# A transformer block on one core: another order for the first transfers, dummy products and transposes

## The chip, the cores and the metric

The kernel runs on one core of a Trainium2 chip. The metric is the device time of one execution, in microseconds; lower is better. Five engines work side by side, each through its own queue in order: TensorE (PE; its weight loads are listed as PEld), VectorE (DVE), ScalarE (ACT), GpSimd (POOL) and SyncE (SP), which only issues transfers here. Transfers from HBM to the on-chip memory are issued by SP, ScalarE or GpSimd and carried by the core's 16 DMA engines.

## What is computed

One layer of a trunk with two token mixers in parallel, float32, 256 tokens of width 2048, with 16 learned meta tokens in front of them:

```
h = concat(meta, x)                              # (16 + 256, 2048)
u = rms_norm(h, g_pre_mix)
z_pool, v_conv, g_conv, gate_a, gate_b = split(u @ w_in)   # 1024 1024 1024 2048 2048
y_a = causal_multiscale_pool(z_pool, w_pool_grp, pool_scale) @ w_pool_out
y_b = conformer_conv(v_conv, g_conv, ...) @ w_conv_out
m = sigmoid(gate_a) * y_a + sigmoid(gate_b) * y_b
h = h + rms_norm(m @ w_o, g_post_mix)
u = rms_norm(h, g_pre_mlp)
h = h + rms_norm(relu(u @ w_up)**2 @ w_down, g_post_mlp)
return h[16:]
```

The change touches the preparation of `u` and the first products of `u @ w_in` alone.

## The kernel before

**Precision.** Each float32 weight is split into a rounded high part `hi` (cast on ScalarE, L250) and the rest `lo` (subtraction on VectorE, L253), each activation likewise into `u[..., 0, :]` and `u[..., 1, :]`; a product is hi·hi + hi·lo + lo·hi, three matmuls (`mm3`, L422).

**Streaming.** All weights come as chunks of 1 MB from one list, `stream`, into three rotating buffers `raw`. Each of the first chunks is 8 row groups of 128 by 256 columns of `w_in`, so two chunks hold the 16 row groups (k = 0 to 15) of the first 256 columns. `open_chunk` issues a chunk's transfers; for the first two chunks its argument says how many row groups go in each transfer and on which queue. `pieces_to` splits single row groups of the first three chunks into hi and lo.

**The start.** The order is written out by hand; nothing is scheduled afterwards, so each engine does its instructions in the order of the program. Transfers: SP loads the meta tokens (`m_in`, 16 rows of 8 KB) and ScalarE the gains `g_pre_mix`; then `x` comes in four blocks of 512 columns (block b holds k = 4b to 4b + 3), block 0 with its first 128 tokens on SP and the others on ScalarE; then chunk 0 (one row group on ScalarE, then one, two, two, two on SP), x block 1 on ScalarE, x block 2 on SP, chunk 1 on SP, x block 3 on SP; the small vectors and the conv taps on GpSimd. ScalarE then loads a function table (`warm_up`).

TensorE begins with `keep_warm(8)`, transposes of the identity into a tile `idle` that nobody reads; then `meta_tokens` transposes the meta rows, 16 pieces of 16 by 128, and the gains (`rows_to_columns`, L312), multiplies on VectorE and casts on ScalarE; then `keep_warm(4)`.

**The loop** (L525 to L540) runs k from -4 to 15. For negative k it transposes one x tile each (`x_tile`, two transposes of 128 by 128, L370, called xt0 to xt3 in the text), scales it into `u` (ScalarE L371, VectorE L372) and splits one row group of weights. From k = 0 on it multiplies row group k into two accumulators `acc_v` (six matmuls of 272 columns, called product k), and after each odd k transposes the next two x tiles. So TensorE's order is xt0 to xt3, products 0 and 1, xt4, xt5, products 2 and 3, xt6, xt7, and so on. The norm's factor is applied later, from sums of squares (`sq_tile`), for which the meta rows are read untransposed from `m_in`.

Of the kernel before, what the change touches and what calls it, by code (L numbers as in the profile page):

```python
# [8 lines left out]
F32 = mybir.dt.float32  # L9
F32R = mybir.dt.float32r  # L10
AF = mybir.ActivationFunctionType
# [3 lines left out]
P = 128  # L15
CK = 4
CW = 512
# [83 lines left out]
def hybrid_block(ctx: ExitStack, tc: tile.TileContext, ins: dict, out: bass.AP):  # L101
    nc = tc.nc
    x = ins["x"][0]
    meta = ins["meta"]
    T, D = x.shape
    M = meta.shape[0]
    L = M + T
    NT = T // P
    KD = D // P
# [17 lines left out]
    const = ctx.enter_context(tc.tile_pool(name="const", bufs=1))  # L127
# [3 lines left out]
    tmp = ctx.enter_context(tc.tile_pool(name="tmp", bufs=2))  # L131
# [3 lines left out]
    def f32(ap):  # L135
        return ap.bitcast(F32)

    def acc_tile(name):
        return psA.tile([P, CW], F32, tag="acc", name=name)

    def misc_tile(name):
        return psB.tile([P, CW], F32, tag="misc", name=name)
# [43 lines left out]
    HALF = (2 * CK, CW // 2)  # L186
# [24 lines left out]
    opened = []  # L211
# [13 lines left out]
    def part_tile(tag, n, standing=False):  # L225

        key = f"{tag}{n % 3}"
        room = ready.pop(key) if key in ready else part_room(key, f"{tag}_{n}")
        place = 2 if standing and tag == "hi" else 1
        shift = (place - 1 - 3 * KEYS.index(key)) % 4 * LINE  # L230
        return room[:, shift:shift + CK * CW]

    def open_chunk(first=((2, nc.sync),) * 4):
        n = at["n"]
        at["n"] += 1
        src, (rows, width) = stream[n]
        raw = raws.tile([P, CK * CW], F32, tag="raw", name=f"raw_{n}")
        hi, lo = (part_tile(tag, at["parts"], n in standing_chunks) for tag in ("hi", "lo"))
        at["parts"] += 1
        flat, (raw, hi, lo) = raw, (t.rearrange("p (k c) -> p k c", k=rows) for t in (raw, hi, lo))  # L240
        pieces = rows if n < FIRST + 1 else 1
        k = rows // pieces
        i = 0
        for n_, queue in first if n < FIRST else ((rows, nc.sync),):
            sl = slice(i, i + n_)
            queue.dma_start(raw[:, sl, :], src[:, sl, :])
            i += n_

        def high(sl):
            nc.scalar.copy(hi[:, sl, :], raw[:, sl, :])  # L250

        def low(sl):
            nc.vector.tensor_sub(lo[:, sl, :], raw[:, sl, :], f32(hi[:, sl, :]))  # L253

        def piece(i):
            def f():
                sl = slice(i * k, (i + 1) * k)
                high(sl)
                low(sl)
            return f  # L260
        opened.append((hi, lo, [piece(i) for i in range(pieces)], flat))
# [13 lines left out]
        return opened.pop(0)[:2]  # L275


    ident = const.tile([P, P], F32, name="ident")
    make_identity(nc, ident)
    ones = const.tile([P, P], F32, name="ones")  # L280
# [3 lines left out]
    def warm_up(func):  # L284

        nc.scalar.activation(warm, ones[:, 0:1], func)
# [3 lines left out]
    m_in = big.tile([M, D], F32, tag="a", name="m_in")  # L290
# [9 lines left out]
    def load_rows(queue, *names):  # L300
        rows = tmp.tile([48, P], F32, tag="g", name=f"rows_{names[0]}")
        n = 0
        for name in names:
            v = ins[name][0].rearrange("(k p) -> k p", p=P)
            queue.dma_start(rows[n:n + v.shape[0], :], v)
            n += v.shape[0]
        return rows, n, names[0]

    def rows_to_columns(rows, n, name):

        pv = misc_tile(f"pv_{name}")
        nc.tensor.transpose(pv[:, :n], rows[:n, :], ident[:n, :n])  # L312
        nc.vector.tensor_copy(vecs[:, cols[name]:cols[name] + n], pv[:, :n])

    def col(name, k):
        return vecs[:, cols[name] + k:cols[name] + k + 1]

    def load_x(queue, b, ts=slice(0, NT)):
        sl = slice(b * CW, (b + 1) * CW)
        queue.dma_start(x_in[:, ts, sl], xv[:, ts, sl])  # L320


    nc.sync.dma_start(m_in, meta)
    pre_rows = load_rows(nc.scalar, "g_pre_mix")
    for t, queue in enumerate((nc.sync, nc.scalar)):
        load_x(queue, 0, slice(t, t + 1))
    open_chunk(((1, nc.scalar), (1, nc.sync), (2, nc.sync), (2, nc.sync), (2, nc.sync)))
    load_x(nc.scalar, 1)
    load_x(nc.sync, 2)
    open_chunk()  # L330
    load_x(nc.sync, 3)
    other_rows = load_rows(nc.gpsimd, "pool_scale", "b_dw", "conv_ln_g", "conv_ln_b", "g_pre_mlp")
    taps_in = big.tile([TAPS, CC], F32, tag="c", name="taps_in")
    nc.gpsimd.dma_start(taps_in, w_dw)
    ssq = const.tile([P, NT + 1, XB], F32, name="ssq")
    nc.gpsimd.memset(ssq, 1.0)
    warm_up(AF.Sqrt)

    idle = misc_tile("idle")

    def keep_warm(n):
        for _ in range(n):
            nc.tensor.transpose(idle[:, :P], ident, ident)

    keep_warm(8)

    u = big.tile([P, KD, 2, -(-L // (4 * LINE)) * 4 * LINE], F32R, tag="um", name="u")[:, :, :, :L]

    def meta_tokens():

        pt = acc_tile("xm")[:, :KD * M].rearrange("p (k m) -> p k m", k=KD)
        for k in range(KD):
            nc.tensor.transpose(pt[:, k, :], m_in[:, k * P:(k + 1) * P], ident[:M, :M])
        rows_to_columns(*pre_rows)
        mg = tmp.tile([P, KD, M], F32, tag="v", bufs=5, name="mg")
        g = vecs[:, cols["g_pre_mix"]:cols["g_pre_mix"] + KD]
        nc.vector.tensor_mul(mg, pt, g[:, :, None].broadcast_to([P, KD, M]))
        nc.scalar.copy(u[:, :, 0, :M], mg)  # L360
        nc.vector.tensor_sub(u[:, :, 1, :M], mg, f32(u[:, :, 0, :M]))

    meta_tokens()
    keep_warm(4)

    def x_tile(k):
        pt = acc_tile(f"xt_{k}")[:, :T]
        sl = slice(k * P, (k + 1) * P)
        for t in range(NT):
            nc.tensor.transpose(pt[:, t * P:(t + 1) * P], x_in[:, t, sl], ident)  # L370
        nc.scalar.activation(u[:, k, 0, M:], pt, AF.Copy, scale=col("g_pre_mix", k))  # L371
        nc.vector.scalar_tensor_tensor(  # L372
            u[:, k, 1, M:], pt, col("g_pre_mix", k), f32(u[:, k, 0, M:]),
            op0=ALU.mult, op1=ALU.subtract)

    def sq_tile(b, t):
        sl = slice(b * CW, (b + 1) * CW)
        junk = tmp.tile([P, CW], F32, tag="junk", bufs=1, name=f"sqx_{b}_{t}")
        src, n = (x_in[:, t, sl], P) if t < NT else (m_in[:, sl], M)
        nc.scalar.activation(junk[:n, :], src, AF.Square, accum_out=ssq[:n, t, b:b + 1])  # L380
# [6 lines left out]
        nc.vector.tensor_scalar(q, q, -0.5, 1.5, op0=ALU.mult, op1=ALU.add)  # L387
        nc.vector.tensor_mul(r, r, q)

    rb = const.tile([P, L], F32, name="rb")  # L390
    sc = {}

    def scale_roots():
# [23 lines left out]
    def mm3(acc, hi, lo, act, k, cs, first, last):  # L417


        off = act.shape[3] - acc.shape[1]  # L420
        for n, (w, a) in enumerate(((hi, 0), (hi, 1), (lo, 0))):
            nc.tensor.matmul(acc, w[:, k[0], cs], act[:, k[1], a, off:],  # L422
                             start=first and n == 0, stop=last and n == 2)
# [18 lines left out]
    def acc_tiles(name, n=CW // P):  # L442
        return [acc_tile(f"acc_{name}_{j}") for j in range(n)]
# [68 lines left out]
    def pieces_to(n):  # L512

        while first["split"] < min(n, (FIRST + 1) * HALF[0]):
            c = first["split"] // HALF[0]
            if c == at["n"]:
                open_chunk()
            opened[c][2].pop(0)()
            first["split"] += 1

    first = {"split": 0}
    accs = [acc[:, :L] for acc in acc_tiles("v0", HALF_CW // P)]
    squares = [(b, t) for b in range(XB) for t in range(NT + 1)]
    LEAD = 4
    for k in range(-LEAD, KD):  # L525
        if k < 0:
            x_tile(k + LEAD)

        pieces_to(min(k + LEAD + 1, KD) + 2 * max(k - KD + LEAD + 1, 0))
        if k < 0:  # L530
            continue
        if k >= HALF[0] and k % 2:
            sq_tile(*squares.pop(0))
        for j, acc in enumerate(accs):
            mm3(acc, *opened[k // HALF[0]][:2], u, (k % HALF[0], k), slice(j * P, (j + 1) * P),
                k == 0, k == KD - 1)
        if k % 2:
            for kx in range(k + LEAD - 1, min(k + LEAD + 1, KD)):
                x_tile(kx)
# [183 lines left out]
    for g in range(NG):  # L723
        for j in range(GK):
            q = g * GK + j
            acc = (acc_tile if q < KP - 2 else misc_tile)(f"acc_grp_{q}")[:, :T]
# [48 lines left out]
    for n in range(NB):  # L775
# [4 lines left out]
    m = big.tile([P, LINE + KD * 2 * T], F32R, tag="um", name="m")[:, LINE:].rearrange(  # L780
        "p (k a t) -> p k a t", k=KD, a=2)
# [421 lines left out]
    accs = acc_tiles("up00")  # L1203
# [498 lines left out]
    for e, cs in enumerate(col_halves):  # L1702
        for w, s in ends:
            h = AT[s][0]
# [47 lines left out]
```

## Time and profile before

| what | value |
|---|---|
| median of 3 runs | 1207.66 us (1207.51 to 1208.38) |
| the profiled execution: time, span | 1208.15 us, 1206.4 us |
| mean granted TensorE clock | 0.998 |
| HBM read, written | 235.17 MB, 2.10 MB |
| mean over the span | 197 GB/s |
| transfers by SP's queue | 229.98 MB, 58.2% of 16 engines' span |
| transfers by ScalarE's queue | 1.91 MB, 0.4% |

The span runs from the first to the last instruction of the profiled execution; its time holds the launch around it too. In the profile's rows an engine stands with the line of the kernel that issued the instruction (`L370`), then the operation, the tile it writes `<-` the tiles it reads, and a count. `PE` rows are matmuls, `SPq` and `ACTq` rows are the issue of a transfer by that engine's queue. A row of the chain of waits has its start, its length and what it was. A row of the stages view has the stage, its length, the busy time of PE, PEld, DVE, ACT and POOL with the number of instructions, the granted TensorE clock, the share of the DMA engines' time and GB/s. Times are microseconds from the start of the span.

### The profile page before, as it was taken

Reading aid. Unit: us, or ns where it says so; the run is one execution under the profiler, and the core shown is the slowest. Engines: PE = TensorE matmul, PEld = TensorE weight load, DVE = VectorE, ACT = ScalarE, POOL = GpSimd, SP = SyncE. Lnnn points to the kernel's source line nnn. Section 1 sums busy time; section 2 is a strip of 40 time slices with the busy share of each in tenths; the row PEclk is TensorE's granted clock in tenths of the full one; section 3 lists DMA queues with packets and bytes.
Section 4 is the critical chain, followed back from the end, with each engine's and each line's share of the span. In section 5 each row is a group of like instructions: output and inputs, shape, how many; then the busy total and the mean of one; then the engine's idle time right before and its main releaser. Section 6 shows DMA issues by size and latency. Waiting matters only on the chain.

```text
span 1206.4 us, 15712 instructions
## 1 busy us (share of the span) xinstructions
PE 1195.8 (99%) x6444; PEld 1038.4 (86%) x6444; DVE 974.7 (81%) x1058; ACT 627.6 (52%) x651; POOL 8.3 (1%) x19
## 2 busy tenths in 40 slices
PE   9999999999999999999999999999999999999997
PEld 9999988888888888898888888888888888888886
DVE  6799978999776778688988878778878778888756
ACT  7533344443583454665555564564554555555542
POOL 1000000000000000000000000000000000000000
PEclk9999999999999999999999999999999999999999
DMA  9655555656558578546475674674764764755841
GB/s 289 210 175 175 178 202 180 208 177 207 175 169 280 176 256 262 181 160 221 144 244 174 187 232 158 198 249 141 245 199 156 261 200 149 244 175 178 275 141 70
DMA packets 162038, 238.27 MB, mean 198 GB/s; under 512 B 4033, under 2 KB 91521, under 8 KB 161440
## 3 DMA queue, kind: packets, MB, share of 16 engines
q1 hardware_dynamic: 159120, 229.98, 58.2%
q0 software_dynamic: 1680, 5.40, 1.7%
q10 hardware_dynamic: 1168, 1.91, 0.4%
q8 instruction: 50, 0.82, 0.3%
q14 instruction: 20, 0.16, 0.0%
HBM read 235.17 MB, written 2.10 MB: 197 GB/s over the span
## 4 chain that ended last, share of the span: by engine, by line
PE 99%; DVE 0%; DMA 0%; DVEq 0%; ACT 0%; issue 0%; ACTq 0%
PE bank_u L427 18%; PE acc_gate L682 14%; PE acc_up L1516 14%; PE bank_u L433 9%; PE bank_a L1516 7%; PE o_c L1020 6%; PE bank_b L1516 5%; PE acc_v L422 4%; PE acc_z L422 4%; PE acc_g L422 4%; PE acc_co L682 4%; PE acc_po L682 4%; PE acc_up L427 1%; PE bank_u L1516 1%; PE o_a L1020 1%; PE acc_up L433 1%
## 5 line engine op out<-in xcount | busy, mean ns | idle before, releaser
L427 PE MATMUL bank_u<-m,hi 128*128 128x512 f32 x960 | 329.9, 390 | 0.0
L433 PE MATMUL bank_u<-m,lo 128*128 128x256 f32 x960 | 265.5, 277 | 0.0
L250 ACT CAST hi<-raw 128x2048 fp32r<-128x2048 f32 (+1 forms) x99 | 151.7, 1548 | 188.9 <-PE acc_gate L682 71.5
L1367 DVE TENSOR_TENSOR lo<-raw_m,hi 128x2048 fp32r<-128x2048 f32 x85 | 194.4, 2289 | 59.2 <-ACT hi L1362 59.2
L1362 ACT CAST hi<-raw_m 128x2048 fp32r<-128x2048 f32 x85 | 162.5, 1912 | 138.1 <-PE bank_u L427 76.8
L253 DVE TENSOR_TENSOR lo<-raw,hi 128x2048 fp32r<-128x2048 f32 (+1 forms) x99 | 180.6, 1835 | 44.1 <-ACT hi L250 43.8
L427 PEld LDWEIGHTS bank_u<-m,hi 128*128 128x128 f32 x960 | 180.2, 188 | 37.9
L433 PEld LDWEIGHTS bank_u<-m,lo 128*128 128x128 f32 x960 | 180.3, 188 | 1.6
L682 PE MATMUL acc_gate<-hi,u 128*128 128x512 f32 x512 | 158.6, 390 | 0.0
L1516 PE MATMUL acc_up<-hi,forms 128*128 128x512 f32 x496 | 157.5, 389 | 0.0
L488 DVE SCALAR_TENSOR_TENSOR c<-a,taps,c 128x256 f32<-128x256 f32 x240 | 115.5, 484 | 7.1 <-ACT c L482 0.5
L682 PEld LDWEIGHTS acc_gate<-hi,u 128*128 128x128 f32 x512 | 96.1, 188 | 20.0
L1516 PEld LDWEIGHTS acc_up<-hi,forms 128*128 128x128 f32 x496 | 93.1, 188 | 19.5
L682 PE MATMUL acc_gate<-lo,u 128*128 128x512 f32 x256 | 99.6, 389 | 0.0
L1516 PE MATMUL acc_up<-lo,forms 128*128 128x512 f32 x248 | 96.6, 389 | 0.0
L1367 DVE TENSOR_TENSOR lo<-raw_c,hi 128x2048 fp32r<-128x2048 f32 x29 | 66.4, 2290 | 21.0 <-ACT hi L1362 21.0
L1516 PE MATMUL bank_a<-hi,forms 128*128 128x512 f32 (+1 forms) x256 | 82.0, 383 | 0.0
L1362 ACT CAST hi<-raw_c 128x2048 fp32r<-128x2048 f32 x29 | 55.3, 1908 | 51.1 <-PE bank_u L427 28.1
L1367 DVE TENSOR_TENSOR lo<-raw_a,hi 128x2048 fp32r<-128x2048 f32 x29 | 66.4, 2289 | 18.4 <-ACT hi L1362 18.4
L1362 ACT CAST hi<-raw_a 128x2048 fp32r<-128x2048 f32 x29 | 55.4, 1910 | 42.4 <-PE bank_u L427 17.1
L1020 PE MATMUL o_c<-hi,m 128*128 128x512 f32 x208 | 65.6, 390 | 0.0
L1516 PE MATMUL bank_b<-hi,forms 128*128 128x512 f32 (+1 forms) x200 | 63.7, 382 | 0.0
(303 smaller groups left out, 1857.1 us busy)
## 6 DMA issues: line engine op xcount, KB each, us to landing
raw<-in_w_in_dram SPq DMA_DIRECT2D x54, 1024.0 KB, 5.1
raw_m<-in_w_down_dram SPq DMA_DIRECT2D x37, 1024.0 KB, 5.3
raw_m<-in_w_up_dram SPq DMA_DIRECT2D x33, 1024.0 KB, 6.2
raw_c<-in_w_down_dram SPq DMA_DIRECT2D x14, 1024.0 KB, 5.3
raw_a<-in_w_up_dram SPq DMA_DIRECT2D x13, 1024.0 KB, 6.0
raw_a<-in_w_down_dram SPq DMA_DIRECT2D x13, 1024.0 KB, 5.2
raw_c<-in_w_up_dram SPq DMA_DIRECT2D x12, 1024.0 KB, 6.0
raw_o<-in_w_o_dram SPq DMA_DIRECT2D x10, 1024.0 KB, 7.5
```

Of the source, the lines that this page charges most:

```text
L250: nc.scalar.copy(hi[:, sl, :], raw[:, sl, :])
L253: nc.vector.tensor_sub(lo[:, sl, :], raw[:, sl, :], f32(hi[:, sl, :]))
L422: nc.tensor.matmul(acc, w[:, k[0], cs], act[:, k[1], a, off:], start=first and n == 0, stop=last and n == 2)
L427: nc.tensor.matmul(acc.rearrange("p (a t) -> p a t", a=2)[:, :, ts], hi[:, k[0], cs], act[:, k[1], :, off + ts.start:off + ts.stop], start ...
L433: nc.tensor.matmul(acc[:, :T], lo[:, k[0], cs], act[:, k[1], 0, off:], start=False, stop=stop, skip_group_check=True)
L488: nc.vector.scalar_tensor_tensor(c, conv["a"][:, q, i:i + T], taps[:, q, i:i + 1], c, op0=ALU.mult, op1=ALU.add)
L682: nc.tensor.matmul(acc, act(kk)[:, a_, ts_], w_[:, k, :], start=kk == 0 and n == 0, stop=kk == nk - 1 and n == 2)
L1020: nc.tensor.matmul(acc, form(k, a_), box[w_][:, k, :], start=start and k == 0 and n == 0, stop=stop and k == CK - 1 and n == 2, skip_group ...
L1362: nc.scalar.copy(box["flat"], raw)
L1367: nc.vector.tensor_sub(lo, raw, f32(box["flat"]))
L1516: nc.tensor.matmul(acc, forms[h][:, f, k, a_, :], box[w_][:, k, cs], start=start and k == 0 and n == 0, stop=stop and k == KH - 1 and n == ...
```

## The change

- A tile `rb`, used much later, is allocated first and 128 of its columns are set to one by VectorE. `keep_warm` now multiplies that tile by itself (a float32 product) instead of transposing the identity; seven of them come first instead of eight, and the four later ones come after xt1.
- The meta tokens are loaded as `m_rows`, 256 rows of 128 elements over 128 partitions, and transposed by two transposes of 128 by 128. The cast of the high part moves from ScalarE to VectorE; the low part (`low_of_meta`) is computed after the first x tile. `m_in` is still loaded, later: on SP between chunk 1 and x block 3.
- x block 0 is loaded in four transfers: its first 256 columns (k = 0, 1) by SP and ScalarE, 128 tokens each, then its other 256 columns likewise, ScalarE's after its row group of chunk 0, SP's ahead of its first one. To this end `open_chunk` calls a function where the count of row groups is 0.
- x block 1 is issued by SP, behind chunk 0, instead of by ScalarE. ScalarE's table load follows its four issues as before.
- Product 0 comes after xt1 and the four dummies, ahead of xt2 and xt3; then product 1, xt4, xt5 and the old order.

```diff
@@ -242,6 +242,9 @@
         k = rows // pieces
         i = 0
         for n_, queue in first if n < FIRST else ((rows, nc.sync),):
+            if n_ == 0:
+                queue()
+                continue
             sl = slice(i, i + n_)
             queue.dma_start(raw[:, sl, :], src[:, sl, :])
             i += n_
@@ -275,6 +278,8 @@
         return opened.pop(0)[:2]
 
 
+    rb = const.tile([P, L], F32, name="rb")
+    nc.vector.memset(rb[:, :P], 1.0)
     ident = const.tile([P, P], F32, name="ident")
     make_identity(nc, ident)
     ones = const.tile([P, P], F32, name="ones")
@@ -315,34 +320,44 @@
     def col(name, k):
         return vecs[:, cols[name] + k:cols[name] + k + 1]
 
-    def load_x(queue, b, ts=slice(0, NT)):
-        sl = slice(b * CW, (b + 1) * CW)
+    def load_x(queue, b, ts=slice(0, NT), cs=(0, 2)):
+        sl = slice(b * CW + cs[0] * CW // 2, b * CW + cs[1] * CW // 2)
         queue.dma_start(x_in[:, ts, sl], xv[:, ts, sl])
 
 
-    nc.sync.dma_start(m_in, meta)
+    m_rows = tmp.tile([P, M * KD // P, P], F32, tag="v", bufs=5, name="m_rows")
+    nc.sync.dma_start(m_rows, meta.rearrange("m (k f) -> (m k) f", f=P).rearrange(
+        "(h p) f -> p h f", p=P))
     pre_rows = load_rows(nc.scalar, "g_pre_mix")
-    for t, queue in enumerate((nc.sync, nc.scalar)):
-        load_x(queue, 0, slice(t, t + 1))
-    open_chunk(((1, nc.scalar), (1, nc.sync), (2, nc.sync), (2, nc.sync), (2, nc.sync)))
-    load_x(nc.scalar, 1)
+    load_x(nc.sync, 0, slice(0, 1), (0, 1))
+    load_x(nc.scalar, 0, slice(1, 2), (0, 1))
+    def rest_of_block():
+        load_x(nc.sync, 0, slice(0, 1), (1, 2))
+        load_x(nc.scalar, 0, slice(1, 2), (1, 2))
+    open_chunk(((1, nc.scalar), (0, rest_of_block), (1, nc.sync), (2, nc.sync), (2, nc.sync),
+                (2, nc.sync)))
+    warm_up(AF.Sqrt)
+    load_x(nc.sync, 1)
     load_x(nc.sync, 2)
     open_chunk()
+    nc.sync.dma_start(m_in, meta)
     load_x(nc.sync, 3)
     other_rows = load_rows(nc.gpsimd, "pool_scale", "b_dw", "conv_ln_g", "conv_ln_b", "g_pre_mlp")
     taps_in = big.tile([TAPS, CC], F32, tag="c", name="taps_in")
     nc.gpsimd.dma_start(taps_in, w_dw)
     ssq = const.tile([P, NT + 1, XB], F32, name="ssq")
     nc.gpsimd.memset(ssq, 1.0)
-    warm_up(AF.Sqrt)
 
     idle = misc_tile("idle")
 
     def keep_warm(n):
         for _ in range(n):
-            nc.tensor.transpose(idle[:, :P], ident, ident)
-    keep_warm(8)
+            nc.tensor.matmul(idle[:, :P], rb[:, :P], rb[:, :P], start=True, stop=True)
+    keep_warm(7)
 
 
 
@@ -350,18 +365,21 @@
 
     def meta_tokens():
 
-        pt = acc_tile("xm")[:, :KD * M].rearrange("p (k m) -> p k m", k=KD)
-        for k in range(KD):
-            nc.tensor.transpose(pt[:, k, :], m_in[:, k * P:(k + 1) * P], ident[:M, :M])
+        pt = acc_tile("xm")[:, :KD * M]
+        for h in range(KD * M // P):
+            nc.tensor.transpose(pt[:, h * P:(h + 1) * P], m_rows[:, h, :], ident)
+        pt = pt.rearrange("p (m k) -> p k m", k=KD)
         rows_to_columns(*pre_rows)
         mg = tmp.tile([P, KD, M], F32, tag="v", bufs=5, name="mg")
         g = vecs[:, cols["g_pre_mix"]:cols["g_pre_mix"] + KD]
         nc.vector.tensor_mul(mg, pt, g[:, :, None].broadcast_to([P, KD, M]))
-        nc.scalar.copy(u[:, :, 0, :M], mg)
+        nc.vector.tensor_copy(u[:, :, 0, :M], mg)
+        return mg
+    mg = meta_tokens()
+    def low_of_meta():
         nc.vector.tensor_sub(u[:, :, 1, :M], mg, f32(u[:, :, 0, :M]))
-    meta_tokens()
-    keep_warm(4)
 
     def x_tile(k):
         pt = acc_tile(f"xt_{k}")[:, :T]
@@ -387,7 +405,6 @@
         nc.vector.tensor_scalar(q, q, -0.5, 1.5, op0=ALU.mult, op1=ALU.add)
         nc.vector.tensor_mul(r, r, q)
 
-    rb = const.tile([P, L], F32, name="rb")
     sc = {}
 
     def scale_roots():
@@ -522,18 +539,28 @@
     accs = [acc[:, :L] for acc in acc_tiles("v0", HALF_CW // P)]
     squares = [(b, t) for b in range(XB) for t in range(NT + 1)]
     LEAD = 4
+    def product_of(k):
+        for j, acc in enumerate(accs):
+            mm3(acc, *opened[k // HALF[0]][:2], u, (k % HALF[0], k), slice(j * P, (j + 1) * P),
+                k == 0, k == KD - 1)
     for k in range(-LEAD, KD):
         if k < 0:
             x_tile(k + LEAD)
+        if k == -LEAD:
+            low_of_meta()
 
         pieces_to(min(k + LEAD + 1, KD) + 2 * max(k - KD + LEAD + 1, 0))
+        if k == 1 - LEAD:
+            keep_warm(4)
+            product_of(0)
         if k < 0:
             continue
         if k >= HALF[0] and k % 2:
             sq_tile(*squares.pop(0))
-        for j, acc in enumerate(accs):
-            mm3(acc, *opened[k // HALF[0]][:2], u, (k % HALF[0], k), slice(j * P, (j + 1) * P),
-                k == 0, k == KD - 1)
+        if k:
+            product_of(k)
         if k % 2:
             for kx in range(k + LEAD - 1, min(k + LEAD + 1, KD)):
                 x_tile(kx)
```

## The prediction

> **What bounds the kernel now.** I read the page first: its span and busy table.
>
> ```profile
> span 1206.4 us, 15712 instructions
> PE 1195.8 (99%) x6444; PEld 1038.4 (86%) x6444; DVE 974.7 (81%) x1058; ACT 627.6 (52%) x651; POOL 8.3 (1%) x19
> ```
>
> TensorE is busy for all but 10.6 us, so a change to the start is worth what it shifts the end of a gapless stream of matmuls. The chain of waits of the first 24 us shows that stream beginning:
>
> ```profile
> 0.74 3.08 DMA m_in<-in_meta_dram
> 3.87 1.89 PE xm L355 x16
> 5.86 1.05 PE idle L343 x4
> 6.91 1.71 PE xt L370 x8
> 8.61 2.43 PE acc_v L422 x12
> 11.04 0.44 PE xt L370 x4
> 11.48 1.49 PE acc_v L422 x12
> 18.75 0.44 PE xt L370 x4
> ```
>
> Columns are start, length and what. After the wait for the meta tokens nothing but TensorE is in it: 16 narrow transposes, the gains' transpose, four dummies, the transposes xt0 to xt3, then products. The same work costs twice as much early as late: eight transposes take 1.71 us, four take 0.44 later; twelve products take 2.43 us, then 1.49. The clock column does not show this, it reads 1.00 in both stages, so I read the slow clock from durations:
>
> ```profile
> 8.20:10.40 2.20, 2.20 (x11) 2.20 (x11) 2.20 (x7) 1.94 (x6) 0.00 (x0) 1.00 1.07 287
> 10.40:12.70 2.30, 2.30 (x21) 2.30 (x20) 2.10 (x7) 2.06 (x6) 0.00 (x0) 1.00 1.06 364
> 10.88 0.60 PE L370 MATMUL xt<-ident,x_in 128*128 128x128 f32 x4
> ```
>
> Between 10.4 and 12.7 us 21 matmuls run where 11 ran before. The third row, of the timeline, is my mark: the first transposes of x block 1 (xt4, xt5) are recorded from 10.88. From there both kernels have the same TensorE work in the same order (products 2 and 3, then xt6), so **the time changes by how far this point moves**, plus any new gap behind it.
>
> **Which transfers that point needs.** x block 1 is issued today by ScalarE as its fourth transfer. Issues and landings, from the timeline and the list of DMA issues (last column: us to landing):
>
> ```profile
> m_in<-in_meta_dram SPq DMA_DIRECT2D x1, 128.0 KB, 3.1
> taps_in<-in_w_dw_dram POOLq DMA_DIRECT2D x1, 124.0 KB, 6.0
> 0.73 0.42 ACTq L305 DMA_DIRECT2D rows_g_pre_mix<-in_g_pre_mix_dram  x1
> rows_g_pre_mix<-in_g_pre_mix_dram ACTq DMA_DIRECT2D x1, 8.0 KB, 3.3
> 4.00 0.38 SPq L246 DMA_DIRECT2D raw<-in_w_in_dram  x1
> 1.19 0.44 ACTq L320 DMA_DIRECT2D x_in<-in_x_dram  x1
> x_in<-in_x_dram ACTq DMA_DIRECT2D x1, 256.0 KB, 5.1
> 6.33 0.37 SPq L320 DMA_DIRECT2D x_in<-in_x_dram  x1
> x_in<-in_x_dram SPq DMA_DIRECT2D x1, 512.0 KB, 6.4
> 1.66 0.45 ACTq L246 DMA_DIRECT2D raw<-in_w_in_dram  x1
> raw<-in_w_in_dram ACTq DMA_DIRECT2D x1, 128.0 KB, 5.7
> 2.14 0.46 ACTq L320 DMA_DIRECT2D x_in<-in_x_dram  x1
> x_in<-in_x_dram ACTq DMA_DIRECT2D x1, 512.0 KB, 8.1
> 4.43 0.60 SPq L246 DMA_DIRECT2D raw<-in_w_in_dram  x1
> raw<-in_w_in_dram SPq DMA_DIRECT2D x1, 256.0 KB, 6.9
> ```
>
> x block 1 lands at 2.14 + 8.1 = 10.24, 0.64 before 10.88: nearly tight already. The last piece of weight chunk 0 lands at 4.43 + 6.9 = 11.33. SP's issues follow landings: 4.00 after the gains (0.73 + 3.3 = 4.03), 6.33 after x block 0 (1.19 + 5.1 = 6.29). Counted over both queues in program order, each transfer waits for the one eight before it.
>
> **The change, part by part.** Only the order of transfers ends up on the path.
>
> *Dummy products.* Seven products of a memset tile replace eight transposes, starting about 1.0 instead of 1.35 (a memset on idle VectorE, at most the 0.20 of the memset below, instead of the identity). A float32 product is two recorded matmuls; the nearest row is
>
> ```profile
> 41.84 0.96 PE pb L412 x6
> 1.25 0.20 POOL L281 MEMSET ones<- 128x128 f32 x1
> ```
>
> 0.16 us each at full clock, at most double at the slow one: 14 of them take 2.2 to 4.5 us and end at 3.2 to 5.5. They lie beside the wait for the meta tokens (3.84) and x. The four later ones cost 1.3 to 2.6 us, now behind xt1 instead of ahead of xt0.
>
> *Meta tokens.* Two 128-wide transposes at 1.71/8 = 0.21 each replace 1.89 us: 1.46 us of TensorE saved. The cast goes from ScalarE (about 0.4) to VectorE, and the low half behind the first x tile: some 0.8 us more ahead of product 0 on VectorE, which waits for x meanwhile.
>
> *x block 0 in halves.* 256 KB instead of 512 KB are needed for xt0. It lands at 6.29 today; a half at no less than 1.19 + 3.1 (the latency of the meta tokens, 3.84 - 0.74) = 4.3, no more than 6.3; I take 5.3, in the middle. Product 0 also needs weight piece 0, today at 1.66 + 5.7 = 7.36 at the latest.
>
> *TensorE up to the mark.* At full clock: 5.3 + 0.44 (xt0, xt1) + 1.3 (four dummies) + 0.75 (product 0, half of 1.49) + 0.44 + 0.75 = 9.0. So without the transfers the mark would move from 10.88 to 9.0, a gain of 1.9 us. Even with piece 0 at 7.36, plus 0.4 for its cast and 0.4 for its low half, product 1 ends by about 10.
>
> *x block 1.* It is moved from ScalarE's fourth issue to SP, behind all of weight chunk 0. One queue serves its transfers in order, so it must land after the meta tokens (128 KB), x block 0 (512), chunk 0 (1024), its own 512, the gains (8) and, on the side, GpSimd's 148 (124 of them the conv taps): 2332 KB, 2.39 MB. That very set has landed today when the last piece of chunk 0 does, at 11.33: everything else in it was earlier, and what SP queued next (x block 2) came behind. The DMA engines are not idle meanwhile:
>
> ```profile
> 0.00:2.00 2.00, 0.65 (x3) 0.65 (x4) 0.00 (x0) 0.00 (x0) 1.36 (x8) 1.00 0.26 61
> 2.00:4.00 2.00, 1.46 (x9) 1.06 (x7) 0.00 (x0) 1.36 (x2) 2.00 (x5) 1.00 0.80 161
> 4.00:6.00 2.00, 2.00 (x18) 1.96 (x19) 0.10 (x1) 0.12 (x1) 0.83 (x3) 1.00 0.94 310
> 6.00:8.00 2.00, 2.00 (x11) 2.00 (x11) 1.04 (x4) 1.03 (x3) 0.00 (x0) 1.00 1.08 392
> 8.00:10.00 2.00, 2.00 (x10) 2.00 (x9) 2.00 (x6) 2.00 (x7) 0.00 (x0) 1.00 1.09 285
> ```
>
> (The two last columns: DMA share, GB/s.) Reordering can't shorten a full pipe: I take 11.4 for the landing, 11.45 for the mark, **+0.57 us**. Bounds: by 6.0 the rows give 0.12 + 0.32 + 0.62 = 1.06 of the 2.39 MB; the rest at the best rate, 392 GB/s instead of 285 in 8 to 10, is done at 9.4 with no lag to the landing, mark 9.45, -1.4 us. On the other side, SP may issue x block 1 only when a half of block 0 has landed; at 6.3, with the 6.4 us that SP's 512 KB takes today, that is 12.7, +1.9 us. I choose 11.4 because it is the same bytes measured. x block 2, next in SP's queue, then lands as today, at 6.33 + 6.4 = 12.7, and is wanted two blocks of 0.44 + 1.49 behind the mark, at 15.3.
>
> *Behind the mark.* The meta rows are loaded once more (128 KB, for the squares) on SP, past chunk 1 and ahead of x block 3:
>
> ```profile
> 11.66 0.47 SPq L320 DMA_DIRECT2D x_in<-in_x_dram  x1
> x_in<-in_x_dram SPq DMA_DIRECT2D x1, 512.0 KB, 6.5
> ```
>
> It lands at 18.16, wanted at 18.75; 128 KB at 350 GB/s, between the rates above, are 0.4 us, so 18.5 against 18.75 + 0.57. Hidden; without that margin at most 0.4. The warm-up of ScalarE's table stays behind four issues: nothing. SP's further issues are in the old order, with the same weights.
>
> **Sum.** In the profiled run's own time: 1206.4 + 0.57 = 1207.0 of span, with the 1.75 around it (1208.15 - 1206.4) 1208.7. The median of the runs is 0.49 below the profiled one, so 1207.66 + 0.57 = **1208.2**.
>
> **A rule weighed.** In the trace TensorE works from 3.87 to 8.61 on transposes almost without a gap and products are still slow until about 10.4. The Trainium skill, "TensorE: Matmul & The Clock Gate", Part 4 (PE-mode transpose), says that transposes don't count as activity the way matmuls do, and Part 1 that a busy window of about 3.4 us opens the gate: the trace agrees with the first. By it the dummy products open the clock near 4.5, and the mark, were it set by TensorE, would be the 9.0 above (-1.9 us, 1205.8); the sum by the transfers gives +0.57, since a fast TensorE waits for x block 1 all the same.
>
> **The rivals.** (a) *The transfers come sooner, TensorE nearly sets the mark.* For it: weight packets in 8 to 10 us move at 285 GB/s and at 392 before, so a quieter stage could save up to 1.8 us. Against: the same weights move then. Mark 9.45 to 10.9, in the middle -0.7: 1207.0. (b) *The whole gain arrives*: mark 9.0, 1205.8; needs x block 1 before 9.0, ahead even of the best rate. (c) *Slower: the clock is down when x block 1 comes.* The new order leaves TensorE with up to 2.4 us of waiting (9.0 to 11.4) right after its first products. That waiting can lower the clock:
>
> ```profile
> 1190.00:1197.50 7.50, 7.50 (x57) 7.15 (x55) 5.93 (x16) 1.40 (x5) 0.00 (x0) 1.00 0.28 105
> 1197.70:1201.70 4.00, 0.00 (x0) 0.00 (x0) 3.38 (x10) 0.71 (x3) 0.00 (x0) 1.00 0.21 81
> 1201.75:1206.30 4.55, 0.00 (x0) 0.00 (x0) 1.14 (x3) 0.00 (x0) 0.00 (x0) 0.50 0.58 213
> ```
>
> At the end about 4 us of nothing pass until the granted clock is 0.50, and the wait here is shorter. A block of four transposes and twelve products is 1.93 us at full clock, about 3.9 at half; one such block slow adds 1.9: +0.57 + 1.9 = +2.5, 1210.1. It decides once the slow stage reaches 2 us behind the mark. The same page of the Trainium skill, Part 1, puts the fall at one idle window of about 3.4 us: by that the wait here is too short, and no run here shows a shorter one. (d) *A later block is late* (x block 3 by more than its margin): +1 to +2.5, 1209 to 1210.
>
> **How the numbers follow.** Forecast 58%, (a) 25%, (b) 4%, (c) 9%, (d) 4%. The forecast's own range is 1207.7 to 1209.6 (mark 10.9 to 12.75). With most of (a), the range is 1206.5 to 1209.6. What a measurement can tell is about 0.2%, 2.4 us: faster than 1205.2 needs the mark under 8.5, under (b)'s own figure, so 4% for all of it with what is unforeseen; slower than 1210.1 has most of (c) and some of (d), 9%; the rest, 87%, is within.
>
> **What would show it.** Right: a gap on TensorE ahead of xt4, released by the DMA of x_in; xt4 near 11.4; the first twelve products in about 1.5 us; the chain naming x_in where it names m_in now. Wrong: no gap there and xt4 under 10 (a, b); products behind the gap at 2.4 us per twelve (c); a gap at 19 us (d). It would also be wrong if x block 1 lands well ahead of the last piece of chunk 0, out of the order of its queue.

## The result, and the profile after

The change made the kernel slower: 1211.11 us median of 10 runs (1209.87 to 1211.58), against 1208.07 (1206.91 to 1208.95) for the kernel before beside it, a ratio of 1.0024, 95% interval [1.0015, 1.0032]. The forecast was 1208.2, with a range up to 1209.6. The profiled execution took 1211.31 us, 3.16 more than the one of before. Its page, span and busy table:

```profile
span 1209.2 us, 15712 instructions
PE 1195.9 (99%) x6440; PEld 1038.3 (86%) x6440; DVE 974.8 (81%) x1060; ACT 627.5 (52%) x650; POOL 8.3 (1%) x19
```

TensorE is as busy as before; idle time in the span grew from 10.6 to 13.3 us. The timeline of TensorE after the change shows the start:

```profile
1.05 3.35 PE L358 MATMUL idle<-rb 128*128 128x128 f32 x14 [1.05 <-DVE rb L282]
4.20 0.59 PE L370 MATMUL xm<-ident,m_rows 128*128 128x128 f32 x2
4.89 0.66 PE L388 MATMUL xt<-ident,x_in 128*128 128x128 f32 x4
5.39 1.06 PE L358 MATMUL idle<-rb 128*128 128x128 f32 x8
6.85 0.52 PE L439 MATMUL acc_v<-u,hi 128*128 128x272 f32 x2 [0.41 <-ACT hi L253]
8.98 0.29 PE L439 MATMUL acc_v<-u,lo 128*128 128x272 f32 x1
11.97 1.09 PE L388 MATMUL xt<-ident,x_in 128*128 128x128 f32 x4 [2.71 <-DMA x_in<-in_x_dram]
```

The dummy products end at 4.40, xt0 starts at 4.89 instead of 6.70, and product 1 is done at 8.98 + 0.29 = 9.27. Then the bracket of the last row: 2.71 us without work, ended by the transfer of x block 1. The mark (xt4) is at 11.97, 1.09 later than the 10.88 of before. The chain of waits after the change says what set it, and what followed:

```profile
1.22 3.20 DMA x_in<-in_x_dram
4.44 0.37 SPq L249
4.85 6.99 DMA x_in<-in_x_dram
11.97 1.09 PE xt L388 x4
13.06 2.37 PE acc_v L439 x12
15.43 0.44 PE xt L388 x4
15.86 1.50 PE acc_v L439 x12
```

SP issued x block 1 at 4.85, and 6.99 us later, at 11.84, it was there. The first block behind it took 1.09 + 2.37 us, the next one 0.44 + 1.50, as every later one. The stages of the profile after (columns as in the prediction: the clock is third from the end) show why:

```profile
4.65:11.40 6.75, 4.21 (x30) 3.54 (x29) 5.03 (x14) 3.59 (x10) 0.17 (x2) 1.00 1.04 327
8.05:11.40 3.35, 1.22 (x11) 1.00 (x9) 2.21 (x6) 2.04 (x6) 0.00 (x0) 1.00 1.04 352
11.50:14.80 3.30, 2.83 (x13) 2.86 (x14) 1.58 (x4) 1.50 (x4) 0.00 (x0) 0.50 1.12 338
14.90:17.20 2.30, 2.30 (x21) 2.30 (x21) 1.01 (x3) 1.44 (x4) 0.00 (x0) 1.00 1.02 224
```

The granted clock is 1.00 up to 11.4, 0.50 from 11.5 to 14.8 (13 matmuls in 3.30 us) and 1.00 again (21 in 2.30). In the clock's records it falls at 11.45, 2.2 us into the wait, and rises at 14.87, 3.41 us later; in the 3.35 us ahead of the fall TensorE was busy for 1.22, 36%.

xt6 is then at 15.26 instead of 12.80 (+2.46), and from there nothing is gained or lost but 0.11: the last product starts at 1199.74 instead of 1197.39. First after, then before:

```profile
1199.74 0.28 PE L1543 MATMUL bank_b<-hi,forms 128*128 128x256 f32 x1
```

```profile
1197.39 0.28 PE L1516 MATMUL bank_b<-hi,forms 128*128 128x256 f32 x1
```

So the 3.16 us of the two profiled executions are: the mark 1.09, the slow block 2.46 - 1.09 = 1.37, less the 0.11; the tail from the last product to the end of the span 9.18 instead of 8.71, 0.47; and the time around the span 2.11 instead of 1.77, 0.34. Of after's ten runs three took 1209.87 to 1210.14 at a mean granted clock of 0.997 or 0.998, seven 1210.95 to 1211.58, all at 0.996; 3.4 us at half clock are 0.0014 of the span, so I take the three for runs in which the clock stayed up (they were not profiled).

### The profile page after: what moved, and what is told of

It reads as the page before. It is cut to its first block, busy times and chain, and to the rows that moved or that the text cites. A ratio compares the mean times of both kernels' runs of the same rounds, so it can differ in the third digit from the quotient of the medians.

```text
span 1209.2 us, 15712 instructions
## 1 busy us (share of the span) xinstructions
PE 1195.9 (99%) x6440; PEld 1038.3 (86%) x6440; DVE 974.8 (81%) x1060; ACT 627.5 (52%) x650; POOL 8.3 (1%) x19
## 4 chain that ended last, share of the span: by engine, by line
PE 98%; DMA 1%; DVE 0%; DVEq 0%; ACT 0%; issue 0%; ACTq 0%; SPq 0%
PE bank_u L444 18%; PE acc_gate L709 14%; PE acc_up L1543 14%; PE bank_u L450 9%; PE bank_a L1543 7%; PE o_c L1047 6%; PE bank_b L1543 5%; PE acc_z L439 4%; PE acc_g L439 4%; PE acc_v L439 4%; PE acc_co L709 4%; PE acc_po L709 4%; PE acc_up L444 1%; PE bank_u L1543 1%; DMA x_in<-in_x_dram 1%; PE o_a L1047 1%
```

## The experiments

All ratios are against the kernel before, run beside; the job's medians stand in brackets.

**1. x block 1 back on ScalarE (from after).**

```diff
         load_x(nc.scalar, 0, slice(1, 2), (1, 2))
+        load_x(nc.scalar, 1)
...
-    load_x(nc.sync, 1)
```

> The changed kernel, but x block 1 is issued by ScalarE as its fifth transfer again, instead of by SP behind weight chunk 0. Theory (the loss is the late x block 1 and the clock that falls in the wait for it): x block 1 lands near 10, as before (10.24), the gap ahead of xt4 shrinks from 2.7 us to 1 or less, the twelve products behind it take 1.5 instead of 2.37 us, the mark (first record of xt4) is at 9.6 to 10.3 instead of 11.97: 3 to 4 us faster than the changed kernel, 0.5 to 1.3 us faster than before. Rival (the loss is in the rest of the start, the halves of x, the dummies or the other meta path): no more than 1 us faster than the changed kernel.

Measured: 1210.63 (1208.34), ratio 1.0019 [1.0009, 1.0028]. Timeline of TensorE:

```profile
10.59 0.63 PE L388 MATMUL xt<-ident,x_in 128*128 128x128 f32 x4 [1.00 <-DMA x_in<-in_x_dram]
20.13 0.63 PE L388 MATMUL xt<-ident,x_in 128*128 128x128 f32 x4 [1.17 <-DMA x_in<-in_x_dram]
43.81 1.00 PE L429 MATMUL pb<-diag,ones 16*128 16x16 f32 x6 [0.31 <-DVE diag L423]
```

The mark came 1.4 us sooner than after's, with the clock up, and yet only half a microsecond of it is in the median and 0.3 at the last product (1199.72 instead of 1200.02). The block behind the mark took 2.41 us (10.59 to 13.00) instead of 1.93, TensorE waited 1.17 us for x block 3, and 0.31 for the norm's scales (`diag` on VectorE, `pb` on TensorE). A miss: the place was right, the gain was not.

**2. x block 1 on SP, nothing else (from before).**

```diff
-    load_x(nc.scalar, 1)
+    load_x(nc.sync, 1)
```

> The kernel before with one edit: x block 1 is issued by SP behind weight chunk 0 instead of by ScalarE. Theory: the mark moves from 10.88 to 11.4 to 11.9, as in the changed kernel, but product 1 ends only near 10.8, so the gap is 1 us at most and the clock stays up behind it: 0.5 to 1 us slower than before. Rival (the transfer order alone is the whole loss): 2.5 us slower or more.

Measured: 1209.15 (1208.34), ratio 1.0005 [0.9997, 1.0014]. Timeline:

```profile
11.86 0.63 PE L370 MATMUL xt<-ident,x_in 128*128 128x128 f32 x4 [1.33 <-DMA x_in<-in_x_dram]
```

The mark moves by 0.98, nearly the 1.09 of the whole change, and the last product by 1.03; a wait of 1.33 us is followed by transposes at full speed (0.63). Moving this one transfer makes nearly the whole of the later mark between these traces; how much a mark differs from trace to trace stands in the section on why the prediction was wrong.

**3. The wait filled with dummies (from after).** Ten, and in another run five.

```diff
             product_of(k)
+        if k == 1:
+            keep_warm(10)
```

> The changed kernel with ten more dummy products (2.6 us at full clock) between product 1 and xt4, in the stretch where TensorE waits for x block 1. Theory: the transfers are untouched, the mark stays near 11.97, the clock stays up, the twelve products behind it take 1.5 us: 1.3 to 1.5 us faster than the changed kernel, still 1 to 1.5 us slower than before. Rival (the clock falls for another reason than the wait, or the slow stage costs nothing): same as the changed kernel within 0.4 us.

> The kernel after the change with five dummy products in the wait ahead of x block 1's transposes, half of the ten of the earlier run, so that about 1.4 us of the wait is left. Theory (the clock falls on how much of a 3.41 us window is idle, and the waits of 1.0 to 1.33 us seen so far kept it): the granted clock stays 1.00 behind the wait in the profiled execution, the block there takes 0.6 + 1.5 us, and the median is about 1 us under after, 1210.0 to 1210.3 us against 1208.1 to 1208.3 for before. Rival (any wait with no product in it for over 1.3 us drops the clock): 0.50 behind the wait, 1.1 + 2.4 us for the block, median 1211 us.

Measured with ten: 1210.01 (1208.34), ratio 1.0013 [1.0005, 1.0022]; with five: 1210.02 (1208.12), 1.0014 [1.0005, 1.0023]. Timelines, ten first:

```profile
9.22 2.39 PE L358 MATMUL idle<-rb 128*128 128x128 f32 x20
11.78 0.63 PE L388 MATMUL xt<-ident,x_in 128*128 128x128 f32 x4 [0.16 <-DMA x_in<-in_x_dram]
```

```profile
8.91 1.28 PE L358 MATMUL idle<-rb 128*128 128x128 f32 x10
11.38 0.63 PE L388 MATMUL xt<-ident,x_in 128*128 128x128 f32 x4 [1.19 <-DMA x_in<-in_x_dram]
```

Work that nobody reads, put where TensorE waits anyway, makes the kernel 1.1 us faster than after by the medians (1.4 against the before of each job): the transposes behind it take 0.63 us instead of 1.09, and the last product ends 1.32 sooner, at 1198.70, with 0.19 of it from a sooner mark. All transfers and all other work are in the order of after, so **the gain is the clock's**. Half the filling does about as much; none of the 11 runs with five is above 1210.32.

**4. The dummies' kind.** Products instead of transposes in the kernel before (shown, shortened); transposes instead of products, the same edit backwards, in the one after.

```diff
-            nc.tensor.transpose(idle[:, :P], ident, ident)
+            nc.tensor.matmul(idle[:, :P], rb[:, :P], rb[:, :P], start=True, stop=True)
```

> The kernel before with one edit: the dummies are float32 products of a memset tile (seven, then four) instead of transposes of the identity (eight, then four). Theory: products raise the clock and transposes don't, so it is up near 5 us instead of 10.5; products 0 and 1 take 1.5 instead of 2.43 us, and the mark is set by x block 1 as it lands today, at 10.2 to 10.5: 0.4 to 0.7 us faster than before, with a gap under 1 us ahead of xt4. Rival (the kind of dummy doesn't matter): the first twelve products still take about 2.4 us, no change.

> The changed kernel with the old dummies, transposes of the identity (eight, then four), in place of products. Theory: transposes don't raise the clock, so products 0 and 1 run at the slow one and end near 10 to 10.8; the mark stays at 11.9 to 12.1, since x block 1 sets it, and the wait ahead of it shrinks to 1 to 2 us; whether the clock is up behind it depends on where its steps of 3.4 us fall, so 0.8 us faster to 0.5 us slower than the changed kernel. Rival (the kind of dummy doesn't matter): the clock is up by 6 us and the run looks like the changed kernel's.

Measured: before with products 1208.8 (1208.34), ratio 1.0003 [0.9994, 1.0012]; after with transposes 1209.86 (1208.08), 1.0016 [1.0008, 1.0025]. Timelines in that order:

```profile
10.42 0.63 PE L372 MATMUL xt<-ident,x_in 128*128 128x128 f32 x4 [0.58 <-DMA x_in<-in_x_dram]
18.27 0.63 PE L372 MATMUL xt<-ident,x_in 128*128 128x128 f32 x4
```

```profile
7.95 1.06 PE L388 MATMUL xt<-ident,x_in 128*128 128x128 f32 x4
11.25 0.63 PE L388 MATMUL xt<-ident,x_in 128*128 128x128 f32 x4 [1.16 <-DMA x_in<-in_x_dram]
```

In the kernel before, the dummy products do open the clock for the first twelve products (the records of a granted clock of 1.00 begin at 4.48 us instead of 10.47), and the mark comes 0.46 sooner; the last product then ends only 0.14 sooner, and the median shows no gain. In the kernel after, *transposes* as dummies are about 1.2 us faster: the early work is slow (1.06 for four transposes at 7.95), TensorE reaches the wait later, waits 1.16 instead of 2.71, and the clock is up behind it (its records begin at 9.61 instead of 4.63). Three of these 11 runs were at 1210.9 to 1211.3 all the same.

**5. What took experiment 1's gain: no reload of the meta rows (from experiment 1).** The squares of the meta rows read 16 rows of x instead.

```diff
-    nc.sync.dma_start(m_in, meta)
...
-        src, n = (x_in[:, t, sl], P) if t < NT else (m_in[:, sl], M)
+        src, n = (x_in[:, t, sl], P) if t < NT else (x_in[:M, 0, sl], M)
```

> As the run with x block 1 on ScalarE, but the late load of the 16 meta rows is left out; the sums of squares for the meta tokens read 16 rows of x instead, so their norm factors are others. In that run x block 3 landed at 19.99 and TensorE waited 1.17 us for it at 19 us; while the meta rows (16 pieces of 8 KB) are under way, the DMA engines move 125 to 230 GB/s at full share. Theory: that load slows all transfers; without it x block 3 lands by 18.7, the gap at 19 us is under 0.3, and TensorE's last product ends 1 to 1.5 us earlier than in that run (1199.72). Rival: only its 128 KB count, 0.4 us, and a gap of 0.7 us or more stays.

Measured: 1209.2 (1208.08), ratio 1.001 [1.0001, 1.0019]. Stage 14 to 16 us of experiment 1, then of this one (the last two columns are DMA share and GB/s):

```profile
14.00:16.00 2.00, 2.00 (x19) 2.00 (x18) 2.00 (x7) 1.88 (x6) 0.00 (x0) 1.00 1.11 274
```

```profile
14.00:16.00 2.00, 2.00 (x19) 2.00 (x18) 2.00 (x7) 1.83 (x7) 0.00 (x0) 1.00 1.08 359
```

The DMA engines are full in both, and move 274 GB/s with the 128 KB of meta rows among the rest, 359 without. Issue and landing of x block 3, from the lists of DMA issues: 11.72 + 8.3 us there, 10.20 + 7.4 here. So 1.5 of the 2.4 us are the earlier issue and 0.9 the shorter way; the wait at 19 us is gone. One wait was left, in this experiment's timeline:

```profile
42.36 1.00 PE L428 MATMUL pb<-diag,ones 16*128 16x16 f32 x6 [0.33 <-DVE diag L422]
```

The scales from the sums of squares are ready 0.94 us later than in before (the last `diag` is done at 42.21 instead of 41.27, and `pb` starts at 42.36 instead of 41.77), although the mark came 0.97 sooner. On the way ScalarE waited for weights, 0.56 us up to 22.19 and 0.31 up to 28.09, which it does not in before. The last product ends at 1198.20, 0.53 later than in before, close to the 0.59 of `pb`.

**6. The tail: more transfers.** Five chunks in the middle of the kernel in halves (from after, shown), three (from before, `n < 23`).

```diff
+        halves_ = ((rows // 2, nc.sync),) * 2
-        for n_, queue in first if n < FIRST else ((rows, nc.sync),):
+        for n_, queue in first if n < FIRST else halves_ if 20 <= n < 25 else ((rows, nc.sync),):
```

> The changed kernel; five weight chunks in the middle of the projections (numbers 20 to 24) are loaded in two halves each, so that the kernel has 8 transfers more than before instead of 3 on the two hardware queues. Theory: at the end SP waits for the transfers' semaphores in a fixed order, about 0.06 us each; with 3 more transfers the three last outputs stand first in that order and the rest comes after them, with 8 more they stand last again: the time from the last product to the end of the span falls from 9.18 to 8.7, the kernel is 0.4 to 0.8 us faster than the changed one, everything else equal. Rival: the tail is something else, 9.2 as before and the same time.

> The kernel before with three chunks in the middle of the kernel loaded in two halves each: three transfers more, as the change has, and nothing else changed. Theory (the tail grew by 0.46 us because three more transfers shift the order in which SP waits for the last landings): the tail from the last product to the end of the span goes from 8.71 us to about 9.2 us, the last product ends where it did (1197.6 us, within 0.2), and the median is 0.4 to 0.8 us above before. Rival (the longer tail comes from something else in the change): tail 8.7 us, median as before within 0.2 us.

Measured: 1210.4 (1208.08), ratio 1.0015 [1.0006, 1.0024], and 1208.1 (1208.12), 1.0001 [0.9992, 1.001]. With the kernel of experiment 8, in the profiled executions:

| kernel | transfers more than before | last product ends | span | tail |
|---|---|---|---|---|
| before | 0 | 1197.67 | 1206.38 | 8.71 |
| before, x block 0 in four (8) | 2 | 1197.51 | 1206.63 | 9.12 |
| before, three halved (6) | 3 | 1197.31 | 1206.31 | 9.01 |
| after | 3 | 1200.02 | 1209.20 | 9.18 |
| after, five more halved (6) | 8 | 1199.65 | 1208.47 | 8.82 |

The tail follows the number of transfers, whatever they carry; the other kernels fit in: 8.72 with none more (2 and the first of 4), 9.15 to 9.17 with three (1, 3, the second of 4, the first of 8), 9.23 with two (5), 8.82 with eight (7). At the end SP waits for the semaphores of all transfers (counters that tell what has landed), one wait after the other in a fixed order, about 0.06 us each: in before one wait is left when the last output lands (1205.49), in after six (landing at 1208.00, the six from 1208.01 to 1208.31). Which transfer has which semaphore goes round in eights, so three more transfers put the last outputs early in the order, and eight more put them back. The 0.30 of the walk is shown in the tail (the other 0.16 are ahead of the last landing); in the median of the second kernel it is not (its last product was 0.36 sooner in the profile), so what it is worth in time stays open.

The kernel with five chunks in halves also repeats the start of after. Its clock fell too, at 11.36, behind a shorter wait:

```profile
11.42 1.09 PE L389 MATMUL xt<-ident,x_in 128*128 128x128 f32 x4 [2.26 <-DMA x_in<-in_x_dram]
```

Six of its 11 runs took 1210.4 to 1211.02 at a mean clock of 0.996 or 0.997, five 1208.86 to 1209.71 at 0.998, so most likely this fall too comes in some executions only.

**7. All repairs at once (from experiment 1).** The five halved chunks, the meta rows' reload behind chunk 2 instead of ahead of x block 3, and their squares last (shortened: the halving is as in 6).

```diff
-    squares = [(b, t) for b in range(XB) for t in range(NT + 1)]
+    squares = [(b, t) for b in range(XB) for t in range(NT)] + [(b, NT) for b in range(XB)]
...
+    nc.sync.dma_start(m_in, meta)
     project(u, KD, first_g, "g0", mm=mm3, width=L, fill=2.4)
```

> The changed kernel with x block 1 issued by ScalarE, the meta rows for the squares loaded behind weight chunk 2 (and squared last), and the five chunks in two halves. Theory: the mark is near 10.6, no slow clock behind it, no gap at 19 us over 0.4, the tail 8.7: between 0.7 us faster than before and 0.3 slower, 2.5 to 3.5 us faster than the changed kernel. Rival (something else in the new start costs): 1 us or more slower than before.

Measured: 1209.75 (1208.08), ratio 1.0014 [1.0005, 1.0023]. Its last wait is the largest of its kind, from the timeline:

```profile
42.50 1.00 PE L429 MATMUL pb<-diag,ones 16*128 16x16 f32 x6 [0.54 <-DVE diag L423]
```

A miss: no sum of repairs beats the kernel before, and I found no version that does.

**8. Other parts alone.** x block 1 ahead of the last 512 KB of chunk 0 on SP (from after); x block 0 in four transfers (from before).

```diff
-    open_chunk(((1, nc.scalar), (0, rest_of_block), (1, nc.sync), (2, nc.sync), (2, nc.sync),
-                (2, nc.sync)))
+    open_chunk(((1, nc.scalar), (0, rest_of_block), (1, nc.sync), (2, nc.sync), (0, lambda: load_x(nc.sync, 1)),
+                (2, nc.sync), (2, nc.sync)))
...
-    load_x(nc.sync, 1)
```

> The kernel after the change with x block 1 issued by SP ahead of the last two transfers of chunk 0 (512 KB), all else as it is. Theory (x block 1 lands when the bytes queued ahead of it have landed, about 327 to 410 KB per us): it lands 1.2 to 1.4 us sooner, at 10.3 to 10.7 us, the wait ahead of its transposes falls from 2.7 us to at most 1.4 us, the clock stays 1.00 behind it, and the last product ends 1 to 2 us sooner than after's 1200.0 us, if the weight pieces moved back or x block 3 do not take it again; median 1209 to 1210.1 us. Rival (x block 1's landing is set by its own queue and not by the bytes ahead): it lands at about 11.8 us again, clock 0.50 behind it, median 1211 us.

> The kernel before with x block 0 in four transfers as in the change (its first 256 columns by both queues, then the others), and nothing else changed; x block 1 is then the fifth issue of ScalarE. Theory: the first transposes of x are not worth anything by themselves here, since four meta and gains steps and the slow clock set them; the mark stays within 0.5 us of 10.88, two transfers more move the tail by 0.1 to 0.3 us, and the median is within 0.5 us of before. What lies outside the span (1.78 us in before, 2.03 to 2.15 us in every kernel with the whole change) tells which part the 0.3 us go with: 2.1 us if with these transfers, 1.8 us if with the meta rows' load, the only part not run alone then. Rival for the mark: x block 1 as fifth issue comes 0.5 to 1 us later, as it did at 10.59 for a TensorE that was sooner, and the median is 0.5 to 1 us above before.

Measured: 1210.02 (1208.12), ratio 1.0014 [1.0005, 1.0023], and 1208.72 (1208.1), 1.0006 [0.9997, 1.0015]. Timelines in that order:

```profile
10.04 0.63 PE L387 MATMUL xt<-ident,x_in 128*128 128x128 f32 x4 [0.74 <-DMA x_in<-in_x_dram]
19.23 0.63 PE L387 MATMUL xt<-ident,x_in 128*128 128x128 f32 x4 [0.98 <-DMA x_in<-in_x_dram]
```

```profile
10.14 0.51 PE L428 MATMUL acc_v<-u,hi 128*128 128x272 f32 x2 [0.34 <-ACT hi L253]
11.21 0.60 PE L376 MATMUL xt<-ident,x_in 128*128 128x128 f32 x4
```

Issued at 3.29 instead of 4.85, x block 1 is there 1.9 us sooner and the clock stays up, but x block 3 is late instead: of the 1.9 us and of the 1.4 for the clock 1.2 are left at the last product (1198.82). Each order tried serves one block at the cost of another. x block 0 in four transfers gains nothing for the mark (11.21): a piece of weights is late there. Its time around the span is 1.79 us as in before (1.77 in this job), while the kernels with the wide load of the meta rows have 1.91 to 2.15 (medians). That points at this load, but it was not run alone, nor were the new place of product 0 and the cast on VectorE; and of the runs with five halved chunks (6), which have the load too, some are as low as 1.76. Where the 0.3 come from stays open.

## Why the prediction was wrong

**Right.** TensorE's side of the sum: the dummies, the two wide transposes and xt0 bring product 1's end to 9.27 where 9.0 was forecast, and the early products ran at full clock (0.29 for one). The gain of it was indeed not had, since TensorE waits for x block 1: the gap, its releaser and the chain naming x_in are as forecast. No wait at 19 us came in after itself, and the later blocks run in the old rhythm.

**The term for the mark was too small for the profiled execution**: +0.57 forecast, 1.09 measured, 0.98 for that edit alone. The step was "That very set has landed today when the last piece of chunk 0 does, at 11.33". From the start to that point the DMA engines moved (before, then after up to its landing)

```profile
0.00:11.33 11.33, 9.43 (x54) 9.00 (x55) 4.28 (x12) 5.35 (x14) 4.19 (x14) 1.00 0.86 258
```

```profile
0.00:11.84 11.84, 7.80 (x45) 6.92 (x45) 5.20 (x15) 5.08 (x12) 4.19 (x14) 0.98 0.84 257
```

at the same mean rate, so 11.33 x 258 = 2.92 MB and 11.84 x 257 = 3.04 MB, both well over the 2.39 MB of the set. The bytes ahead give only the earliest time, not the landing: transfers issued later were moved meanwhile, and 0.12 MB more of them after the change. The sixteen parts of x block 1 land between 10.02 and 11.84, those of chunk 0's last piece in before between 10.15 and 11.37. The Trainium skill, "DMA: Bandwidth & Descriptors", section "Why a DMA increments its semaphore by 16 and not by 1", says that a transfer is split over up to sixteen engines that finish independently, and is done with the last; this spread of 1.8 us agrees.

But 11.84 is also the latest of its kind. In the four other traces with the same first transfers (both of experiment 3, the second kernel of 4, the first of 6) x block 1 landed at 11.11 to 11.64; with after's the mean is 11.42, what the forecast had. The marks there are 11.25 to 11.97, and with the start of before unchanged 10.28 (the second kernel of 6) and 10.88. So about half a microsecond of a mark is the execution's, and the comparison of two traces can't tell how much of the 0.52 is the term's.

**Rival (c) was the case**: the forecast gave it 9% and +1.9 for the slow block; 1.37 was measured, as the slow stage ended 2.9 us behind the mark, and the sign named for it, 2.4 us per twelve products behind the gap, came as 2.37. Its +2.5 for mark and block together met the measured 2.46 by luck, with a mark 0.52 too small and a block 0.53 too large. The step that failed is "about 4 us of nothing pass until the granted clock is 0.50, and the wait here is shorter". The wait was 2.71 us, longer than the 2.4 by the late mark and shorter than that stretch, and it sufficed. Nor was the late mark needed for it: in experiment 6 a wait of 2.26 us ahead of a mark at 11.42, where the forecast had it, was enough. The row of 4 us at the end only showed that so much is enough. Experiments 1 to 5, 7 and 8 set waits of 0.16 to 1.33 us ahead of the mark, and the profiled clock stays up behind each; behind 2.26 and 2.71 it falls, and filling the wait (experiment 3) keeps it up. The Trainium skill, "TensorE: Matmul & The Clock Gate", Part 1, counts activity in free-running windows of 3.4 us and has the clock fall after one idle window. The 3.41 us from fall to rise agree; an idle window was not needed, since the 3.35 us ahead of the fall were 36% busy. Where between 1.33 and 2.26 us the limit lies, and how far it depends on the phase, was not tried; that some runs of after kept the clock speaks for a part of the phase.

**Terms that were not in the sum**: the tail, 0.47, and the time around the span, 0.34. The forecast counted the three more transfers as work at the start and took the end and "the 1.75 around it" as they were. For the reload of the meta rows, "Hidden; without that margin at most 0.4" held in after only because the mark was late: with a sooner mark (experiments 1 and 8) the wait for x block 3 is 1.17 and 0.98 us, and without the reload it is gone (5). Most of the rest of the miss is the comparison's own: the before beside after ran at 1208.07, not at the 1207.66 of three runs that the sum started from.

## What to carry to other kernels

Making an engine reach a wait sooner was worth nothing here and had a cost: an earlier TensorE waited longer, and the longer wait halved its clock for the block behind it. Size a moved transfer from landings measured in its new place in the queue, in more than one execution; the bytes ahead of it give only the earliest time. Count the transfers that an edit adds at the end of the kernel too, not only where they are issued.

## What the runs showed of the hardware that was not expected

- The clock fell 2.2 us into a wait of 2.71 us and of one of 2.26 us (experiment 6), with the 3.4 us ahead of the fall 36% busy in both. Dummy products in the wait are worth 1.1 us (1210.01 against 1211.11), and slower dummies ahead of it 1.2.
- A load of 16 rows of 8 KB slows all transfers beside it while the DMA engines stay full: 274 GB/s against 359 in the two stages of experiment 5. Where experiment 7 loads the rows later, the slow stretch comes later too: 362 GB/s in 14 to 16 us, 222 in 20 to 22, at shares of 1.09 and 1.08.
- The tail depends on the number of transfers by 0.3 to 0.5 us (8.71 us with none more, 9.01 to 9.23 with two or three, 8.82 with eight), 0.30 of it through the order of SP's last waits.
